# A fp32 decoder layer on one Trainium2 core: the FFN's two products as seven block products over pairs of token tiles, and its sample rows as plain fp32 products on four column strips

## The chip, the cores and the metric

The kernel runs on one core of a Trainium2 chip, as one launch. The metric is the device time of one execution in microseconds (us). Before the change it is 2831.03 us, the median of three runs (2824.38 to 2838.37). All inputs and outputs are fp32.

## The reference

One layer of a hybrid decoder for 2048 prompt tokens and 32 sample rows (8 requests of 4 tokens). A mixer (differential attention and retention on one normalised input) is followed by the FFN with which this case deals. Width D is 1024, D_FF is 2816.

```python
def swiglu(h, w_in_l, w_out_l):
    g, u = jnp.split(h @ w_in_l, 2, axis=-1)
    return (jax.nn.silu(g) * u) @ w_out_l

xp = xp + merge_head_groups(diff_o, ret_o, rg, ...)          # mixer, D wide
xp = xp + swiglu(rms_norm(xp, norm_ffn_g[l], NORM_EPS), w_ffn_in[l], w_ffn_out[l])
y_prompt = rms_norm(xp, norm_final_g, NORM_EPS)              # the same for xs, y_sample
```

## The kernel before

TensorE computes a fp32 product as **three fp32r products**. `split` (L114) makes two operands of one: `hi`, the fp32 value cast to fp32r by ACT (L116), and `lo`, what is left, by a DVE subtraction (L117). Then hi·hi, lo·hi and hi·lo are added up in PSUM.

The program has three stages. `projection` takes the input products of all rows (0 to about 600 us). `mixer` runs attention and retention over tiles of 128 tokens, and lays pieces of `out_rows` between attention pieces: for each tile it takes the out projection (L941 to L943), the residual, the FFN's norm (`stats`, `weigh`), and in `finish` turns the tile (four TensorE transposes into one PSUM tile, twice, in `turn`, L879), splits it and stores hi and lo to DRAM (`x2t_d`, POOL's queue, L975). `ffn` (L1014) is the rest.

`ffn` goes over four **groups of 512 tokens**; the fourth has the 32 sample rows too (544 columns, cut into two pieces of 272). For each group:

- `ffn_in` loads the group's hi and lo (L1041, POOL's queue). For each of 22 column tiles `f` of D_FF, and for gate and up, it loads 512 KB of weights (L1048, SP's queue), splits them, and takes 8 contraction steps `k` of three products (L1061): weights of 128x128 stand, 512 tokens move. SiLU is on ACT (L1066), the multiplication on DVE (L1067). The hidden rows `ht` stay in SBUF.
- `ffn_out` takes each half of the output's columns: for each `f` it loads 256 KB of weights, splits these and `ht`, and takes three products of 512 columns for each of four tiles of tokens (L1111 to L1113), which add up in four PSUM tiles over all 22 `f`. The sample rows go as one 64-row product of hi and lo together (`sample_terms`, L299). Residual (L1120), square (L1124), a power on POOL (L1156), scaling (L1157, L1158) and the store (L1161) follow for each tile. In the last group the last six `f` are held back, so that the tiles end one after the other.

A scheduler puts the order of the instructions of each engine down before the run, from the program's dependencies and a model of their times; buffers that run through rings (`bufs=`) set how far ahead a load or a split may go. The PSUM ring of the FFN has two pools of four.

The change and the prediction touch `out_rows`, `ffn`, `ffn_in`, `ffn_out` and the ring.

## Time and profile before

| | |
|---|---|
| runs | 2824.38, 2831.03, 2838.37 us |
| the profiled execution | 2826.33 us, of which the span from its first to its last instruction is 2824.6 us |
| granted TensorE clock, mean of the span | 0.997 |
| projection | 0 to about 600 us |
| mixer with `out_rows` | about 600 to 1246 us |
| FFN | about 1246 us to the end |
| DMA | 387.44 MB, mean 137 GB/s |

The page of the profile gives each engine's busy time and a strip of the span in 40 slices; its chain of waits follows the work that ended last back to the start. PE is the matrix engine (TensorE), DVE, ACT and POOL are the vector, scalar and GpSimd engines, SP is the queue that issues most loads. A matmul's own duration is not what it costs: matmuls overlap, and what counts is the distance from one start to the next, which the chain and the timeline show. Times at 1246 us and after belong to the FFN, apart from the last tiles of `out_rows`, whose products stand between the first FFN products up to about 1375 us.

### The profile page before, as it was taken

How to read it: one execution, taken by the hardware profiler on the slowest of the kernel's cores; microseconds unless marked ns; L12 is line 12 of the kernel's file. 1: busy time of each engine (PE TensorE's matmuls, PEld its weight loads, DVE VectorE, ACT ScalarE, POOL GpSimd, SP SyncE). 2: the span in 40 equal slices, each digit the busy share in tenths (PEclk: the TensorE clock that was granted, in tenths of full speed). 3: DMA queues.
4: the chain of work that ended last, by engine and by line, in shares of the span. 5: the costliest groups of instructions: out<-in, count | busy, mean ns of one | idle time of the engine just before them, and what ended most of it. 6: DMA issues, size and time to landing. Idle time of an engine off the chain costs nothing.

```text
span 2824.6 us, 37296 instructions
## 1 busy us (share of the span) xinstructions
PE 2777.2 (98%) x14584; PEld 2291.0 (81%) x14584; DVE 1296.6 (46%) x2198; ACT 1076.9 (38%) x2067; POOL 297.4 (11%) x421
## 2 busy tenths in 40 slices
PE   8999999999988999999999999999999999999998
PEld 7777788886667888888888888888888888999977
DVE  5454444444666776743322453224432235322254
ACT  4343343433565665642322442223432234322243
POOL 1000000004641221121000000000000000000000
PEclk9999999999999999999999999999999999999999
DMA  7436364356984766475633525335253342422122
GB/s 248 114 116 199 110 198 123 123 153 186 254 216 112 171 151 155 103 217 146 190 95 92 161 91 167 92 95 161 75 183 90 97 164 90 163 87 86 49 79 88
DMA packets 200784, 387.44 MB, mean 137 GB/s; under 512 B 20432, under 2 KB 88704, under 8 KB 200608
## 3 DMA queue, kind: packets, MB, share of 16 engines
q1 hardware_dynamic: 112240, 267.11, 30.2%
q0 software_dynamic: 79152, 113.75, 16.7%
q10 hardware_dynamic: 9216, 4.20, 0.6%
q8 instruction: 115, 1.88, 0.3%
q14 instruction: 61, 0.50, 0.1%
HBM read 311.72 MB, written 73.27 MB: 136 GB/s over the span
## 4 chain that ended last, share of the span: by engine, by line
PE 94%; ACT 2%; DVE 2%; DMA 1%; issue 1%; POOL 0%; ACTq 0%; POOLq 0%; SPq 0%
PE fps L1061 35%; PE z L290 6%; PE z L289 6%; PE z L288 6%; PE fps L1112 6%; PE fps L1113 6%; PE fps L1111 6%; PE op L840 4%; PE sp L782 2%; PE atp L829 2%; PE sp L785 2%; PE cz L941 2%; PE cz L942 2%; PE cz L943 2%; DMA cat<-cat_d 1%
## 5 line engine op out<-in xcount | busy, mean ns | idle before, releaser
L1061 PE MATMUL fps<-fx,fwh 128*128 128x512 f32 (+1 forms) x3520 | 896.3, 351 | 0.0
L1061 PEld LDWEIGHTS fps<-fx,fwh 128*128 128x128 f32 x3520 | 595.2, 188 | 94.7
L1061 PE MATMUL fps<-fx,fwl 128*128 128x512 f32 (+1 forms) x1760 | 562.0, 352 | 0.0
L116 ACT CAST fwh<-fwr 128x1024 fp32r<-128x1024 f32 x176 | 184.6, 1049 | 695.4 <-PE fps L1061 663.3
L117 DVE TENSOR_TENSOR fwl<-fwr,fwh 128x1024 fp32r<-128x1024 f32 x176 | 215.6, 1225 | 350.2 <-ACT fwh L116 342.6
L1061 PEld LDWEIGHTS fps<-fx,fwl 128*128 128x128 f32 x1760 | 308.0, 188 | 46.1
L288 PE MATMUL z<-wh,xh 128*128 128x512 f32 x768 | 303.6, 397 | 7.9 <-ACT xh L182 7.9
L290 PE MATMUL z<-wl,xh 128*128 128x512 f32 x768 | 304.4, 397 | 0.0
L289 PE MATMUL z<-wh,xl 128*128 128x512 f32 x768 | 302.8, 395 | 0.0
L1112 PE MATMUL fps<-vh,hl 128*128 128x512 f32 x680 | 263.4, 390 | 0.0
L1113 PE MATMUL fps<-vl,hh 128*128 128x512 f32 x680 | 263.2, 390 | 0.0
L1111 PE MATMUL fps<-vh,hh 128*128 128x512 f32 x680 | 206.1, 389 | 0.0
L786 DVE TENSOR_REDUCE mx<-sp 128x1 f32<-128x1024 f32 (+4 forms) x192 | 168.3, 907 | 70.3 <-PE sp L785 54.8
L1067 DVE TENSOR_TENSOR ht<-fps,sg 128x512 f32<-128x512 f32 (+1 forms) x110 | 63.0, 589 | 296.8 <-PE fps L1061 296.8
L117 DVE TENSOR_TENSOR vl<-vr,vh 128x512 fp32r<-128x512 f32 x170 | 117.1, 690 | 171.8 <-ACT vh L116 171.5
L116 ACT CAST vh<-vr 128x512 fp32r<-128x512 f32 x170 | 105.6, 622 | 201.3 <-PE fps L1112 195.7
L288 PEld LDWEIGHTS z<-wh,xh 128*128 128x128 f32 x768 | 145.0, 189 | 38.0 <-ACT xh L182 7.9
L290 PEld LDWEIGHTS z<-wl,xh 128*128 128x128 f32 x768 | 145.0, 189 | 31.8 <-issue 0.7
L289 PEld LDWEIGHTS z<-wh,xl 128*128 128x128 f32 x768 | 145.0, 189 | 31.2 <-issue 0.3
L117 DVE TENSOR_TENSOR wl<-wr,wh 128x1024 fp32r<-128x1024 f32 x96 | 117.3, 1223 | 110.3 <-ACT wh L116 109.9
L1111 PEld LDWEIGHTS fps<-vh,hh 128*128 128x128 f32 x680 | 127.6, 188 | 29.0
L782 PE MATMUL sp<-kst,qd 128*128 128x512 f32 (+1 forms) x320 | 125.8, 393 | 25.3 <-ACT p L800 19.3
(267 smaller groups left out, 3789.4 us busy)
## 6 DMA issues: line engine op xcount, KB each, us to landing
fwr<-w_ffn_in SPq DMA_DIRECT2D x176, 512.0 KB
wr<-w_in SPq DMA_DIRECT2D x96, 512.0 KB
vr<-w_ffn_out SPq DMA_DIRECT2D x176, 256.0 KB
kst<-k_d POOLq DMA_DIRECT2D x36, 512.0 KB
qd<-q_d POOLq DMA_DIRECT2D x64, 256.0 KB
fx<-x2t_d POOLq DMA_DIRECT2D x24, 512.0 KB
vv<-v_d SPq DMA_DIRECT2D x36, 256.0 KB
xr<-xt SPq DMA_DIRECT2D x16, 512.0 KB
```

The lines of the kernel that those rows point to most:

```text
L116: nc.scalar.copy(hi, src)
L117: nc.vector.tensor_tensor(lo, src, hi.bitcast(F32), ALU.subtract)
L288: mm(z, h[:, j, c], wh[:, j], start=k == 0, stop=False)
L289: mm(z, l[:, j, c], wh[:, j], start=False, stop=False)
L290: mm(z, h[:, j, c], wl[:, j], start=False, stop=k == KT - 1)
L782: nc.tensor.matmul(sp[:, o : o + nn], q[:, 2 * mp, sl], k, start=True, stop=False)
L786: nc.vector.tensor_reduce(mx[:, c : c + 1], sp[:, :w], AX.X, ALU.max, negate=True)
L840: self.nc.tensor.matmul(st["o"], ats[(b - lo) // 4][:, (b - lo) % 4, :], vs[b // 4][:, b % 4, :], start=b == 0, stop=b == st["i"],)
L1061: nc.tensor.matmul(pt[:, : c1 - c0], w[:, k], x[:, j, c0:c1], start=first, stop=last)
L1111: nc.tensor.matmul(o, hh[:, sl], vh, start=f == 0, stop=False)
L1112: nc.tensor.matmul(o, hl[:, sl], vh, start=False, stop=False)
L1113: nc.tensor.matmul(o, hh[:, sl], vl, start=False, stop=f == NF - 1)
```

## The change

The prompt's tokens are taken in pairs of 128-token tiles, even and odd. With X = [X11 X12; X21 X22] (rows: even and odd tile; columns: the two halves of the contraction) and W = [W11 W12; W21 W22], X·W comes from **seven block products instead of eight** (Winograd's form of Strassen's scheme):

- operands of X: X11, X12, X22 and the sums S1 = X21 + X22, S2 = S1 - X11, S3 = X11 - X21, S4 = X12 - S2; of W: W11, W21, W22 and four differences in the same manner
- products 0 to 6, each over half the contraction, then sums of the products for the four blocks of the result.

**FFN in** (`ffn_in`): two halves of 1024 tokens, four pairs each, so that 512 columns move as before. Columns of W are paired as gate and up. For each half, `x` has 28 tiles (7 operands, 4 contraction steps) of hi and lo, in SBUF for the whole half, with one buffer each; they are loaded raw through four single buffers `so0` to `so3` (L1102) and split. Their sums are made in `out_rows` (`sums`, POOL) and stored as fp32 (`xop_d`, SP's queue). For each `f` one load of 1 MB (ring `w` of 2), four POOL differences, seven splits into a ring of 8, and seven products of 4 steps by 3 terms (L1139). ACT, DVE and POOL add the products up. The column tiles are taken in pairs f = j and f = j + 11, whose hidden rows are the operands of FFN out; after each pair POOL makes four sums in `so0` to `so3` and stores seven operands (`hop_d`).

**FFN out** (`ffn_out`): for each of seven products in turn, 11 steps `j` of 8 pairs of tiles by 3 terms (L1302 to L1307), into 8 PSUM banks; each step loads 512 KB of `hop_d` and 256 KB of weights by SP and splits them. The differences of these weights (`top_d`) are made by POOL in the second half of FFN in (`second`), one `j` at a time. Each product ends with adds on DVE, ACT and POOL; the residual rows (`x2_d`) stay in SBUF.

**Sample rows**: for each `f` of the first half, 8 plain fp32 products of 32 rows by 256 columns, on four strips of 32 rows of the PSUM tile (`sample_in`), and two small products with a constant that adds the strips up and turns them (`sample_mid`); in `second`, four more on strips for FFN out.

The core of the diff, with pools, tile names and the plain loads cut:

```diff
@@ out_rows @@
         def finish(t):
...
-            hi = cr.tile([P, KT, P], F32R, tag="xhi", name="xhi", bufs=1)
-            lo = cr.tile([P, KT, P], F32R, tag="xlo", name="xlo", bufs=1)
+            xt = cr.tile([P, KT, P], F32, tag="xt", name="xt", bufs=2)
             for q in range(2):
-                self.turn(ps, r["xn"], m, q, hi, lo)
-            g = min(t // 4, 3)
-            c = P * t - 512 * g
-            for s, src in ((0, hi), (1, lo)):
-                nc.gpsimd.dma_start(self.x2t_d[g][s, :, :, c : c + m], src[:, :, :m])
+                tp = ps.tile([P, 4, P], F32, tag="t", name="ctp", bufs=2)
+                for j in range(4):
...
+                    nc.tensor.transpose(tp[:, j, :m], r["xn"][:m, c : c + P], self.ident[:m, :m])
+                dst = xt[:, 4 * q : 4 * q + 4, :m]
+                if q:
+                    nc.vector.tensor_copy(dst, tp[:, :, :m])
+                else:
+                    nc.scalar.copy(dst, tp[:, :, :m])
...
+            if t % 2 == 0:
+                self.even = xt
+                nc.sync.dma_start(d[0][:, :, c], xt[:, :half])
+                nc.sync.dma_start(d[1][:, :, c], xt[:, half:])
+                return
+            nc.sync.dma_start(d[3][:, :, c], xt[:, half:])
+            self.odd = (t, xt)
+
+        def sums():
...
+            tt = nc.gpsimd.tensor_tensor
+            tt(a22, a21, a22, ALU.add)
+            tt(a21, a11, a21, ALU.subtract)
+            tt(a11, a22, a11, ALU.subtract)
+            tt(a12, a12, a11, ALU.subtract)
+            for o, src in ((4, a22), (6, a21), (5, a11), (2, a12)):
+                nc.sync.dma_start(d[o][:, :, c], src)
@@ ffn_in @@
+            def operands(g):
...
+                for o in (0, 4, 5, 6, 1, 2, 3):
+                    for k in range(half):
+                        r = line(f"so{n % 4}")
+                        n += 1
+                        nc.sync.dma_start(r, self.xop_d[g][o][:, k, :])
...
+                        self.split(h, l, r)
...
+            def weights(w):
...
+                tt = nc.gpsimd.tensor_tensor
+                put(0, w11)
+                t1, t2, t3, t4 = (line("wt", 4) for _ in range(4))
+                tt(t1, w12, w11, ALU.subtract)
+                put(4, t1)
...
+            def sample_in(f, w):
+                z = psf.tile([P, 512], F32, tag="sz", name="sz", bufs=1)
+                for b in range(2):
+                    for q in range(4):
+                        k = 4 * b + q
+                        nc.tensor.matmul(
+                            z[32 * q : 32 * q + 32, : 2 * P].rearrange("p (s c) -> p s c", s=2),
+                            xs[:, k, :],
+                            w[:, :, k, :],
+                            start=b == 0,
+                            stop=b == 1,
+                        )
...
+            for g in range(2):
+                x = operands(g)
+                for j in range(NF // 2):
+                    hh = []
+                    for e in range(2):
+                        f = j + e * (NF // 2)
...
+                        ws = weights(w)
+                        ba, bb, bc_, bd = (ring.tile() for _ in range(4))
+                        product(0, ba, x, ws, True)
+                        c1 = line("c1")
+                        nc.scalar.copy(c1, ba)
+                        product(4, bc_, x, ws, True)
...
+                        if g == 0:
+                            z, zs = sample_in(f, w)
+                        product(5, bb, x, ws, True)
+                        u2 = line("u2")
+                        nc.vector.tensor_tensor(u2, bb, c1, ALU.add)
+                        product(6, bd, x, ws, True)
+                        u3 = line("u3")
+                        nc.vector.tensor_tensor(u3, bd, u2, ALU.add)
+                        nc.gpsimd.tensor_tensor(c5, u3, c5, ALU.add)
+                        if g == 0:
+                            sample_mid(f, z, zs)
+                        product(1, ba, x, ws, False)
...
+                        product(2, bc_, x, ws, False)
...
+                        product(3, bd, x, ws, False)
...
+                    so = [line(f"so{n}") for n in range(4)]
+                    tt = nc.gpsimd.tensor_tensor
+                    tt(so[0], h21, h22, ALU.add)
+                    tt(so[1], so[0], h11, ALU.subtract)
+                    tt(so[2], h11, h21, ALU.subtract)
+                    tt(so[3], h12, so[1], ALU.subtract)
+                    d = self.hop_d[j]
+                    for o, src in enumerate((h11, h12, so[3], h22, so[0], so[1], so[2])):
+                        nc.gpsimd.dma_start(d[o][:, g, :], src)
+                    if g == 1:
...
+                        self.second(fw, line, j, acc)
+    def second(self, fw, line, j, acc):
...
+        for n in range(2):
+            for e in range(2):
+                q = 2 * n + e
+                nc.tensor.matmul(
+                    acc[32 * q : 32 * q + 32, :],
+                    self.hs[:, j + e * (NF // 2), :],
+                    w[:, e, 512 * n : 512 * n + 512],
...
+        tt(t[0], w12, w11, ALU.subtract)
+        tt(t[1], w22, t[0], ALU.subtract)
+        tt(t[2], w22, w12, ALU.subtract)
+        tt(t[3], w21, t[1], ALU.subtract)
+        for n in range(4):
+            nc.gpsimd.dma_start(self.top_d[j][:, n, :], t[n])
@@ ffn_out @@
+            def operands(o, j):
+                xr = fo.tile([P, 2, 512], F32, tag="xr", name="xr", bufs=3)
+                nc.sync.dma_start(xr, self.hop_d[j][o])
+                wr = fo.tile([P, 512], F32, tag="wr", name="wr", bufs=4)
...
+                x = self.halves(fo, xr.rearrange("p g t -> p (g t)"), 1024, ("xh", "xl"), 4)
+                return *x, *self.halves(fo, wr, 512, ("vh", "vl"), 4)
...
+            for o, fresh in ((0, True), (1, False), (5, True), (4, True), (2, False), (6, True), (3, False)):
+                if fresh:
+                    banks = [ps.tile([P, 512], F32, tag="ps", name="ops") for _ in range(8)]
...
+                for j in range(nj):
+                    parts = operands(o, j)
+                    if o == 3 and j >= nj - last:
+                        held.append((j, parts))
+                        continue
+                    for p in range(8):
+                        product(banks[p], p, *parts, fresh and j == 0, j == nj - 1)
...
+                    if o == 0:
+                        nc.scalar.copy(u, b)
+                    elif o == 1:
+                        add(xa[p][:, lo], b, xa[p][:, lo], ALU.add)
+                    elif o == 5:
+                        add(u, b, u, ALU.add)
+                        padd(xa[p][:, hi], u, xa[p][:, hi], ALU.add)
...
```

How the rows of the engines move, at three places. Names carry a number of the buffer; a row's end is the size of the result.

First **PE where `out_rows` ends and the FFN begins**: before, the first rows of the FFN (`fps`, L1061) stand among the out projections (`cz`) and the turning (`ctp`) of the last tiles:

```order
L943 MATMUL cz_11331<-wol7_6663,chi_11300 128x512
L879 MATMUL ctp_11375<-ident_84,xn_11273 128x128 x4
L879 MATMUL ctp_11422<-ident_84,cat_11327 128x128 x4
L1061 MATMUL fps_12019<-fx00_11997,fwh_12015 128x512
L1061 MATMUL fps_12050<-fx00_11997,fwh_12046 128x512
L1061 MATMUL fps_12085<-fx00_11997,fwh_12081 128x512
L941 MATMUL cz_11384<-woh0_5496,chi_11300 128x512
L942 MATMUL cz_11384<-woh0_5496,clo_11301 128x512
L943 MATMUL cz_11384<-wol0_5497,chi_11300 128x512
```

After, the last out projection and the last turning stand ahead of the first row of the FFN (L1139):

```order
L947 MATMUL cz_12026<-woh7_6764,chi_11968 128x512
L948 MATMUL cz_12026<-woh7_6764,clo_11969 128x512
L949 MATMUL cz_12026<-wol7_6765,chi_11968 128x512
L979 MATMUL ctp_12060<-ident_180,xn_12054 128x128 x4
L979 MATMUL ctp_12066<-ident_180,xn_12054 128x128 x4
L1139 MATMUL fps_12313<-xh00_12109,wh_12277 128x512
L1139 MATMUL fps_12473<-xh00_12109,wh_12437 128x512
L1139 MATMUL fps_12313<-xl00_12110,wh_12277 128x512
L1139 MATMUL fps_12313<-xh00_12109,wl_12278 128x512
L1139 MATMUL fps_12313<-xh01_12115,wh_12277 128x512
L1139 MATMUL fps_12473<-xl00_12110,wh_12437 128x512
```

Before, 264 rows of the out projections of the last tiles follow the first row of the FFN; after, none does, and the first two `f` run side by side.

Second, **POOL during FFN in**. Before, it issues the loads of a group's operands and takes the powers of the norm:

```order
L1041 DMA fx12_14525<-x2t_d1_76 128x2x512
L1041 DMA fx02_14523<-x2t_d1_76 128x2x512
L1041 DMA fx13_14529<-x2t_d1_76 128x2x512
L1041 DMA fx03_14527<-x2t_d1_76 128x2x512
L1156 TENSOR_TENSOR fss_13967<-fss_13967,half_90 128x1
```

After, in the second half of the tokens (`wt` the weights' differences, `so` the sums of hidden rows, L1253 to L1258 `second`):

```order
L1129 TENSOR_TENSOR wt_17255<-w_17246,wt_17253 128x512
L1253 TENSOR_TENSOR wt_17413<-w2_17406 128x512
L1216 TENSOR_TENSOR so1_17068<-so0_17067,h00_16902 128x512
L1221 DMA hop_d2_4_108<-so0_17067 128x512
L1254 TENSOR_TENSOR wt_17414<-w2_17406,wt_17413 128x512
L1258 DMA top_d3_170<-wt_17413 128x512
L1255 TENSOR_TENSOR wt_17415<-w2_17406 128x512
L1218 TENSOR_TENSOR so3_17070<-h10_17047,so1_17068 128x512
L1221 DMA hop_d2_5_109<-so1_17068 128x512
L1195 TENSOR_TENSOR c5_17169<-u3_17197,c5_17169 128x512
L1258 DMA top_d3_170<-wt_17414 128x512
```

So POOL has sums of 512 columns that it did not have, and the stores are issued between them.

Third, **SP at the boundary of the two halves of tokens**. Before, its rows at such a place are loads of the next weights and of what FFN out needs. After:

```order
L1102 DMA so0_15960<-xop_d1_0_82 128x512
L1102 DMA so2_16116<-xop_d1_3_85 128x512
L1102 DMA so1_15966<-xop_d1_0_82 128x512
L1102 DMA so0_15984<-xop_d1_4_86 128x512
L1102 DMA so3_15978<-xop_d1_0_82 128x512
L1102 DMA so1_15990<-xop_d1_4_86 128x512
L1102 DMA so0_16008<-xop_d1_5_87 128x512
L1102 DMA so3_16002<-xop_d1_4_86 128x512
```

The operands of the second half pass through the same four single buffers in which POOL makes the sums of hidden rows.

More of the change, by code (lines that the diff above doesn't have):

```diff
@@ L1002, in out_rows @@
             yield
+            sums()
             product(t, 1, range(4, 8))
@@ L1012, in out_rows @@
         yield
+        sums()
     def ffn(self):
[L1015 to L1030 removed]
@@ new lines, in ffn, with pool @@
+        tc, nc, a = self.tc, self.nc, self.a
+        with ExitStack() as st:
+            def pool(name, **k):
+                return st.enter_context(tc.tile_pool(reuse_waits="tile", name=name, **k))
+            fs = pool("fs", bufs=1, side="right")
+            self.hs = fs.tile([P, NF, NS], F32, name="hs")
+            self.comb = fs.tile([P, NS + P], F32, name="strips")
+            nc.gpsimd.dma_start(self.comb, a["strips"])
+            self.ysum = fs.tile([NS, D], F32, name="ysum")
+            self.ffn_in()
+            self.ffn_out()
@@ new lines, in second @@
+    def second(self, fw, line, j, acc):
+        nc, a = self.nc, self.a
+        w = fw.tile([P, 2, D], F32, tag="w", name="w2", bufs=2)
+        for e in range(2):
+            nc.sync.dma_start(w[:, e, :], a["w_ffn_out"][j + e * (NF // 2)])
+        for n in range(2):
+            for e in range(2):
+                q = 2 * n + e
+                nc.tensor.matmul(
+                    acc[32 * q : 32 * q + 32, :],
+                    self.hs[:, j + e * (NF // 2), :],
+                    w[:, e, 512 * n : 512 * n + 512],
+                    start=j == 0,
+                    stop=j == NF // 2 - 1,
+                )
+        w11, w12, w21, w22 = w[:, 0, :512], w[:, 0, 512:], w[:, 1, :512], w[:, 1, 512:]
+        t = [line("wt", 4) for _ in range(4)]
+        tt = nc.gpsimd.tensor_tensor
+        tt(t[0], w12, w11, ALU.subtract)
[4 more added lines that the diff above has]
+            nc.gpsimd.dma_start(self.top_d[j][:, n, :], t[n])
@@ L1187, with __init__ @@
 class _Ring:
-    def __init__(self, *pools):
-        self.pools, self.n, self.first = pools, 0, True
+    def __init__(self, four, three):
+        self.pools, self.n = [four] * 4 + [three] * 3, 0
     def tile(self):
-        pool = self.pools[0 if self.first else self.n // 4 % 2]
+        n = self.n % 7
         self.n += 1
-        return pool.tile([P, 512], F32, tag="ps", name="fps")
+        return self.pools[n].tile([P, 512], F32, tag="ps", name="fps", bufs=4 if n < 4 else 3)
 class _Tag:
@@ L1258, in tables @@
     c["dsel"] = ds
+    st = np.zeros((P, NS + P), f)
+    st[p, p % NS] = 1.0
+    for n in range(2):
+        st[p, NS + NS * n + p % NS] = p // (2 * NS) == n
+    c["strips"] = st
     c["piota"] = np.arange(P, dtype=f)[:, None]
```

325 lines of the change are left out of this document (180 added, 145 removed).

## Prediction

> **What bounds the kernel now.** I read the page first, then the chain, then windows of the FFN.
>
> ```profile
> span 2824.6 us, 37296 instructions
> ...
> PE 2777.2 (98%) x14584; PEld 2291.0 (81%) x14584; DVE 1296.6 (46%) x2198; ACT 1076.9 (38%) x2067; POOL 297.4 (11%) x421
> ...
> GB/s 248 114 116 199 110 198 123 123 153 186 254 216 112 171 151 155 103 217 146 190 95 92 161 91 167 92 95 161 75 183 90 97 164 90 163 87 86 49 79 88
> ...
> PE 94%; ACT 2%; DVE 2%; DMA 1%; issue 1%; POOL 0%; ACTq 0%; POOLq 0%; SPq 0%
> ```
>
> PE is busy for 98% of the span, and 94% of the chain of waits is PE's. Busy spans overlap on PE, so I check stage by stage. The windows give the length, then busy time and instructions of PE, PEld, DVE, ACT and POOL, the granted clock, the DMA share and GB/s.
>
> ```profile
> 1040.00:1240.00 200.00, 199.11 (x1281) 172.31 (x1280) 141.75 (x223) 121.33 (x267) 35.73 (x56) 1.00 0.56 144
> 1372.00:1562.00 190.00, 190.00 (x821) 153.47 (x820) 58.31 (x60) 48.15 (x60) 6.00 (x9) 1.00 0.42 125
> 1562.00:1682.00 120.00, 120.00 (x531) 99.31 (x530) 59.79 (x96) 49.90 (x91) 1.40 (x2) 1.00 0.38 119
> 1684.00:1927.00 243.00, 243.00 (x1048) 196.28 (x1047) 75.94 (x82) 64.89 (x84) 6.48 (x10) 1.00 0.39 122
> 2412.00:2676.00 264.00, 264.00 (x2105) 263.80 (x2104) 79.97 (x114) 68.36 (x115) 2.47 (x4) 1.00 0.32 102
> 2815.00:2825.00 10.00, 2.27 (x10) 1.07 (x8) 3.32 (x7) 2.89 (x6) 1.07 (x2) 0.81 0.25 93
> ```
>
> Up to the tail PE has no gap in the FFN, at a granted clock of 1.00. DVE (75.94 of 243) and ACT (64.89) are far from full, POOL is idle. So the FFN's time is its number of matmuls by their spacing, and a matmul removed is worth one spacing. The chain and PE's timeline give it (start, length, what):
>
> ```profile
> 1628.76 2.31 PE fps L1061 x10
> ...
> 1684.60 242.19 PE fps L1061 x1043
> ```
>
> ```profile
> 2413.22 262.82 PE fps L1061 x2098
> ```
>
> ```profile
> 1561.70 0.39 PE L1111 MATMUL fps<-vh,hh 128*128 128x512 f32 x1
> ...
> 1565.79 0.39 PE L1111 MATMUL fps<-vh,hh 128*128 128x512 f32 x1
> ```
>
> A group of FFN in has 22x2x8x3 = 1056 matmuls of 512 columns. Ten were taken early, so 242.19 us are 1046 matmuls: **0.2315 us** each (the trace lacks three records). The fourth group, 2112 of 272 columns, takes **262.8 us**. In FFN out, 18 matmuls lie between the two starts: 4.09/18 = **0.2275 us**.
>
> **What goes.** FFN in: 3 groups x 1056 x 0.2315 = 733.4, and 262.8. FFN out: 4 groups x 2 halves x 22 f x 4 tiles x 3 = 2112 by 0.2275 = 480.5. Sample rows of FFN out: 88 by the same = 20.0. Together 1496.7 us.
>
> **What comes on PE.** FFN in: 2 halves x 22 f x 7 products x 4 steps x 3 terms = 3696 of 512 columns, x 0.2315 = 855.6. FFN out: 7x11x8x3 = 1848 x 0.2275 = 420.4. For the sample rows the decode part has the same forms:
>
> ```profile
> 736.47 1.92 PE L612 MATMUL dop<-pg,dat 128*32 128x512 f32 x16
> 738.32 0.50 PE L782 MATMUL sp<-kst,qd 128*128 128x512 f32 x1
> ```
>
> ```profile
> 690.50 1.34 PE L543 MATMUL dsn<-ks_t,qb 128*128 128x32 f32 x8
> 691.77 0.41 PE L557 MATMUL dsp<-pg,qb 128*32 128x128 f32 x2
> ```
>
> A plain fp32 product leaves two records. So eight strip products of 512 columns on four strips took 738.32 - 736.47 = 1.85 us; eight of 256 columns take half, 0.93. Four products of 32 columns took 1.27, two 0.64. Per f that is 1.57, by 22 = 34.5; four strip products of 512 columns in each of 11 `second` are 11 x 0.93 = 10.2; the two at the end about 1. Sum added: 855.6 + 420.4 + 45.7 = 1321.7.
>
> **Gain on PE: 1496.7 - 1321.7 = 175.0 us.**
>
> **What must stay under PE.** A pair of column tiles (f = j, j + 11) has 168 matmuls: 38.9 us of PE. With samples this is 42.0 us in the first half; in the second, 39.8.
>
> ```profile
> L117 DVE TENSOR_TENSOR vl<-vr,vh 128x512 fp32r<-128x512 f32 x170 | 117.1, 690 | 171.8 <-ACT vh L116 171.5
> ...
> L116 ACT CAST vh<-vr 128x512 fp32r<-128x512 f32 x170 | 105.6, 622 | 201.3 <-PE fps L1112 195.7
> ```
>
> DVE has 14 split subtractions and 12 further 512-column operations a pair: 26 x 0.69 = 18 us. ACT has 14 casts and 8 others: 22 x 0.62 = 14 us. In FFN out, one step of 24 matmuls is 5.46 us of PE against DVE's 3 x 0.69 and ACT's 3 x 0.62. Its loads are 768 KB, so 144 GB/s; the strip of GB/s above has slices at 248 and 254. All of this is covered.
>
> **POOL** is the engine whose load is new. It gets 14 sums of 512 columns and 7 stores a pair in the first half, 18 and 11 in the second.
>
> ```profile
> L517 POOL MEMSET qb<- 128x1024 f32 x1 | 1.0, 951 | 0.0
> ...
> L111 POOL TENSOR_SCALAR nss<-nss 128x4 f32<-128x4 f32 x16 | 5.7, 357 | 91.9 <-ACT njunk L902 91.9
> ```
>
> ```profile
> L695 POOL DMA_DIRECT2D qd<-q_d x64 | 35.2, 563 | 52.8 <-PE sp L785 52.1 <-PE atp L829 0.6
> L975 POOL DMA_DIRECT2D x2t_d<-xhi x17 | 15.4, 904 | 130.0 <-ACT xhi L116 130.0
> L112 POOL TENSOR_TENSOR css<-css,half 128x1 f32<-128x1 f32 x16 | 8.9, 558 | 1.4
> L111 POOL TENSOR_SCALAR css<-css 128x1 f32<-128x1 f32 x16 | 3.0, 190 | 9.6 <-ACT xn L957 9.6
> ```
>
> No row shows a sum of 512 columns on POOL. Lower end: the memset writes 1024 columns in 0.951, so 0.48 for 512. Upper end: from one column to four, TENSOR_SCALAR grows from 190 to 357 ns, 56 ns a column, 28 us for 512. The memset is the nearer row, as the only wide one. A sum reads two streams and writes one, so I take three times 0.48 = **1.4 us**. A store's issue I take as 0.65, between 0.563 and 0.904. First half: 14 x 1.4 + 7 x 0.65 = 24.2 of 42.0. Second: 18 x 1.4 + 11 x 0.65 = 32.4 of 39.8. Covered, but with a margin of only a fifth.
>
> The Trainium skill, page "GPSIMD Engine Reference", section "3.1 Elementwise — side-by-side cycle accounting", speaks against placing sums there: elementwise work is to go to DVE, since GpSimd needs 4497 ns for an addition of 2048 fp32 columns. An estimate from it for 512 is 1.12 us, and POOL's second half would be 27.4 of 39.8; no run here shows it yet.
>
> **What the change opens on PE** (working values, with their ends):
>
> ```profile
> L963 DVE SCALAR_TENSOR_TENSOR xn<-xres,css,gf 128x1024 f32<-128x1024 f32 x16 | 20.5, 1279 | 5.5 <-POOL css L112 5.5
> ...
> L957 ACT ACTIVATE xn<-xres 128x1024 f32<-128x1024 f32 x16 | 17.0, 1061 | 24.9 <-issue 18.0 <-DVE xres L949 6.9
> ```
>
> ```profile
> 1238.26 4.50 DMA cat<-cat_d
> ```
>
> - **Start of the FFN, +18 (5 to 40).** PE no longer has FFN products between the last tiles. Each of the last four exposes a cast, a subtraction and their signals, about 1.7, so 7. The last tile then has residual 0.69, square 1.06, POOL 0.19 + 0.56, weighing 1.28, two copies and a turning, some 6 in all after what still runs. Its four POOL sums (5.6), store and reload (a landing took 4.50) stand before product 4's operands, and only product 0 of two f's (5.6) covers them: 5.
> - **Boundary of the token halves, +16 (5 to 35).** SP's reloads through `so0` to `so3` wait until POOL has made and stored the last pair's sums there. After the last product: DVE 0.69, SiLU 0.62, DVE 0.69, two sums and some issues 4.8, a store 3, a reload 3, a split 1.3, less the little that is ready. Behind these SP has the next loads, which PE needs later. Then each product of two f's (24 x 0.2315 = 5.6 us) asks for four operands, whose line cycle of about 4.7 is shorter.
> - **FFN in to FFN out, +5 (0 to 12):** the first `hop_d` and weights are long stored; gfin, residual rows and new pools come.
> - **Six changes of product in FFN out, +6 (0 to 12):** each bank is read by one copy or add (0.69) before it is restarted. Where the next product adds to the bank, nothing waits.
> - **Tail, +1 (0 to 4);** attention, where SP's stores of sums stand ahead of its loads, **+2 (0 to 12)**.
> - **Small waits for POOL and DVE, +8 (0 to 25):** weights' differences stand in order among `hop_d` sums and stores, and a split behind a late one holds up a product.
> - **Clock, +5 (0 to 15).** Where PE has gaps the granted clock is lower:
>
> ```profile
> 650.00:700.00 50.00, 43.91 (x248) 32.89 (x247) 21.18 (x68) 14.77 (x50) 15.38 (x18) 0.93 0.57 170
> ...
> 2820.00:2824.60 4.60, 0.00 (x0) 0.00 (x0) 0.74 (x1) 0.72 (x1) 0.54 (x1) 0.63 0.12 29
> ```
>
> Sum of losses: 61. **Result:** the profiled execution took 2826.3 us (span 2824.6), 4.7 below the median of 2831.03, inside the runs' spread. 2826.3 - 175.0 + 61 = 2712, rounded to **2710 us**. The losses' ends add up to 10 and 155; that all lie at one end is unlikely, and I take 25 to 110. With 25, and FFN in at FFN out's spacing (3696 x 0.004 = 15 less), it is 2661; with 110, 2761.
>
> **Rivals.**
>
> A. *DVE and POOL block each other.* A pair has 18 DVE operations with both inputs in SBUF (14 subtractions, 4 products of SiLU or sums): 12.4 us. If POOL's sums wait for these, POOL's second half is 25.2 + 12.4 + 7.2 = 44.8 against 39.8, so 11 x 5.0 = +55: **2765**. The first half, 36.6 of 42, still fits. Against it: in 1040 to 1240 DVE is busy 141.75 of 200 and POOL 35.73, and PE keeps 199.11; but POOL reads little there. The Trainium skill, page "SBUF — State Buffer", section "Who interferes with whom", has such a lock: a DVE instruction with two SBUF inputs contends with a GpSimd instruction that reads SBUF. No run here shows it so far. Chance 0.20.
>
> B. *POOL becomes the bound, and the kernel is slower.* Place: the weights' differences of FFN in, without which product 4 does not start. With d the time of a sum, the second half is bound from 18d + 7.2 > 39.8, d = 1.8, the first from 14d + 4.6 > 42, d = 2.7. The gain of 114 is gone at d = 2.4. At d = 3 the cost is 11 x (21.4 + 4.6) = +286: **2998**. For it: 56 ns a column, and 558 ns for a power of one column. Against: those are narrow rows where fixed cost rules; the memset is wide and fast. Chance 0.12.
>
> C. *The strips do not run side by side.* Each would take 3.7 for four, so 33 products of this kind cost 2.8 more: +91, **2803**. The L612 row speaks against it: it is this form. Chance 0.04.
>
> That the change does less than it says: the counts of matmuls are fixed by the loops, so only their cover is open, which A and B are.
>
> **How the numbers follow.** The forecast has 0.64, A 0.20, B 0.12, C 0.04. The range 2655 to 2805 holds the forecast's own ends, A and C; left out are B and a tail of the forecast. About 0.5% (14 us) is what a measurement can tell from no change. Faster by more holds for forecast, A and most of C, and for B at d below 2.3: 0.84. The same: 0.04, a narrow strip of B. Slower: 0.12.
>
> **What would show it.** PE's spacing in FFN in 0.2275 to 0.2315; POOL's sums near 1.4 us, under 1.8; POOL busy about 80% of the second half (B: 100%, PE waiting for `wt` or `wl`; A: sums of uneven length, longer while DVE runs L117); PE idle about 18 us before the first FFN product and 16 at the boundary; eight strip products in 0.93 us. The prediction is wrong if PE idles in every pair, if the spacing of the matmuls changes with seven operands in turn, or if the boundaries cost several times what I gave them.

## The result and the profile after

The changed kernel takes **2729.01 us** (median of four runs, 2727.98 to 2735.78), before 2831.87 in the same session: a ratio of **0.9643, with a 95% interval of 0.9614 to 0.9671**. The forecast was 2710, range 2655 to 2805. The profiled execution took 2728.34 us, with a span of 2726.6; before, the span was 2824.6, so 98.0 us went.

From the page, the first lines:

```profile
span 2726.6 us, 35659 instructions
...
PE 2616.8 (96%) x13180; PEld 2092.6 (77%) x13180; DVE 1568.0 (58%) x2296; ACT 1061.8 (39%) x2051; POOL 950.8 (35%) x991
```

PE is busy 160.4 us less, but no longer without gaps. Its page's chain of waits cannot be followed back to the start in this trace (PE has only 28% of the span in it), so I read windows. The columns are again length; busy time and instructions of PE, PEld, DVE, ACT, POOL; granted clock; DMA share; GB/s.

```profile
1246.00:1338.00 92.00, 79.14 (x353) 62.46 (x351) 41.33 (x57) 24.84 (x61) 40.77 (x44) 0.93 0.48 155
1338.00:1400.00 62.00, 53.02 (x215) 36.07 (x216) 39.98 (x56) 29.13 (x53) 22.17 (x18) 0.91 0.52 168
1400.00:1800.00 400.00, 400.00 (x2010) 318.05 (x2009) 216.56 (x291) 126.76 (x232) 227.62 (x206) 1.00 0.28 97
...
1816.00:1875.00 59.00, 39.32 (x145) 27.06 (x144) 34.28 (x42) 22.85 (x40) 24.96 (x23) 0.86 0.57 190
1875.00:2270.00 395.00, 394.62 (x1763) 317.78 (x1762) 308.08 (x263) 124.70 (x219) 297.64 (x289) 1.00 0.44 153
...
2282.00:2319.00 37.00, 37.00 (x164) 30.60 (x164) 13.73 (x15) 9.64 (x13) 11.44 (x21) 1.00 1.00 376
2319.00:2330.00 11.00, 0.41 (x3) 0.01 (x1) 0.17 (x2) 2.14 (x4) 2.89 (x2) 0.61 0.44 169
2330.00:2713.00 383.00, 383.00 (x1679) 316.93 (x1680) 183.43 (x203) 131.71 (x181) 61.91 (x45) 0.99 0.47 153
```

The two long stretches of FFN in (400 and 395 us) and FFN out after 2330 are as full as the FFN was before. Apart from the passage from FFN in to FFN out and the tail, PE is idle in four places: at the last tiles of `out_rows`, in the first 62 us of FFN in, at the boundary of the token halves (about 1816 to 1875), and once in FFN out, at 2319.

Of the 2010 records in 1400 to 1800, 1613 are FFN matmuls; the sample rows of 20 column tiles take about 27 us (below), so the spacing is (400 - 27)/1613 = 0.2313 us. In 1875 to 2270, 1689 are FFN matmuls, and nine `second` of 1.0 us each lie among them: (395 - 9)/1689 = 0.2285. The last row has 383/1679 = 0.2281, but its first 5 us stand at half the clock (next section); in the variant e4, whose FFN out has no stop, 1848 matmuls take 419.0 us, 0.2267 each. The sample rows on PE's timeline, with the FFN's next row behind each:

```profile
1508.11 1.07 PE L1153 MATMUL sz<-w,xs 128*32 128x256 f32 x16
1509.12 0.50 PE L1139 MATMUL fps<-xh,wh 128*128 128x512 f32 x1
...
1514.73 0.53 PE L1167 MATMUL sz<-strips,zs 128*128 128x32 f32 x4
1515.09 0.48 PE L1139 MATMUL fps<-xh,wh 128*128 128x512 f32 x1
```

Eight strip products take 1.01 us (0.93 was forecast), the two small ones 0.36 (0.64).

For the comparisons below I cut the FFN at PE's own instructions: the time from the 1st to the 200th matmul of FFN in (**start**), from the 1700th to the 2000th (**boundary**), from the 2000th to the 3600th (**steady**), and from the first to the last matmul of FFN out (**out**). By the spacings and the sample rows without any wait, start would be 50.0, boundary 72.7, steady 375 and out 419. The whole FFN is counted from its first matmul to the end of the span: the stages ahead of it scatter. In the 13 profiled executions of the changed kernel and its variants the FFN began between 1332.2 and 1352.7 us, though no edit was aimed at that. Medians of two variants that differ by less than some 10 us are therefore not told apart by their ratios; the parts of the FFN, each from the one profiled execution, are the firmer comparison. Start scatters too: 64.7 to 71.5 us in variants whose edits were not aimed at it.

| kernel | median us | ratio to before | start | boundary | steady | out | FFN |
|---|---|---|---|---|---|---|---|
| changed | 2729.01 | 0.9643 (0.9614 to 0.9671) | 68.9 | 101.1 | 374.7 | 432.0 | 1388.4 |
| e1_late_norm | 2729.81 | 0.9661 (0.9639 to 0.9683) | 67.1 | 100.1 | 375.1 | 431.8 | 1385.8 |
| e4_norm_tied | 2719.56 | 0.9625 (0.9599 to 0.9651) | 68.0 | 99.1 | 375.4 | 418.8 | 1373.2 |
| e2c_ring_six | 2723.20 | 0.9631 (0.9608 to 0.9654) | 64.7 | 99.7 | 383.5 | 419.4 | 1379.0 |
| e2_own_lines | 2717.75 | 0.9613 (0.9589 to 0.9637) | 65.0 | 79.6 | 385.4 | 430.8 | 1372.5 |
| e3_start | 2733.07 | 0.9664 (0.9641 to 0.9687) | 61.2 | 102.0 | 376.8 | 432.5 | 1386.2 |
| e8_out_eight | 2757.53 | 0.9752 (0.9727 to 0.9777) | 66.0 | 76.6 | 374.9 | 485.3 | 1414.4 |
| e6_twice | 2832.17 | 1.0012 (0.9998 to 1.0025) | 71.5 | 105.8 | 466.1 | 431.5 | 1486.7 |
| e7_dve_diffs | 2732.57 | 0.9665 (0.9639 to 0.9691) | 68.3 | 99.9 | 375.6 | 432.5 | 1388.0 |
| e5_both | 2713.70 | 0.9591 (0.9561 to 0.9621) | 67.1 | 85.2 | 383.3 | 420.9 | 1367.8 |
| e9_best | 2724.26 | 0.9636 (0.9613 to 0.9660) | 68.6 | 88.5 | 386.1 | 420.6 | 1375.7 |
| e11_best_dve | 2716.75 | 0.9589 (0.9573 to 0.9605) | 69.5 | 85.8 | 373.7 | 420.9 | 1362.0 |
| **e12_best_dve_all** | **2705.30** | **0.9552 (0.9533 to 0.9572)** | 68.4 | 81.7 | 373.7 | 420.0 | 1355.6 |

### The profile page after: what moved, and what is told of

Its sections match the earlier page's. It is cut to its first block, busy times and chain, and to the rows that moved or that the text cites. A ratio compares the mean times of both kernels' runs of the same rounds, so it can differ in the third digit from the quotient of the medians.

```text
span 2726.6 us, 35659 instructions
## 1 busy us (share of the span) xinstructions
PE 2616.8 (96%) x13180; PEld 2092.6 (77%) x13180; DVE 1568.0 (58%) x2296; ACT 1061.8 (39%) x2051; POOL 950.8 (35%) x991
## 5 line engine op out<-in xcount | busy, mean ns | idle before, releaser
L1139 PE MATMUL fps<-xh,wh 128*128 128x512 f32 x1232 | 486.9, 398 | 20.0 <-ACT xh L122 19.6
L1139 PE MATMUL fps<-xl,wh 128*128 128x512 f32 x1232 | 483.3, 393 | 3.4 <-DVE xl L123 3.4
L1139 PE MATMUL fps<-xh,wl 128*128 128x512 f32 x1232 | 481.0, 391 | 0.0
L1139 PEld LDWEIGHTS fps<-xh,wh 128*128 128x128 f32 x1232 | 232.5, 189 | 89.9 <-ACT xh L122 25.3
L1139 PEld LDWEIGHTS fps<-xl,wh 128*128 128x128 f32 x1232 | 232.7, 189 | 57.0 <-DVE xl L123 9.3
L1139 PEld LDWEIGHTS fps<-xh,wl 128*128 128x128 f32 x1232 | 232.6, 189 | 49.3 <-issue 0.4
L123 DVE TENSOR_TENSOR wl<-wt,wh 128x512 fp32r<-128x512 f32 x176 | 218.4, 1246 | 77.7 <-ACT wh L122 73.1
L1305 PE MATMUL ops<-vh,xh 128*128 128x512 f32 x616 | 234.1, 391 | 12.7 <-ACT xh L122 10.6
L1305 PE MATMUL ops<-vh,xl 128*128 128x512 f32 x616 | 239.3, 391 | 0.0
L1305 PE MATMUL ops<-vl,xh 128*128 128x512 f32 x616 | 239.1, 390 | 0.0
```

The source lines that it names most:

```text
L123: nc.vector.tensor_tensor(lo, src, hi.bitcast(F32), ALU.subtract)
L1139: nc.tensor.matmul(bank, w[:, c], v, start=first and k == 0 and n == 0, stop=k == half - 1 and n == 2, skip_group_check=True,)
L1305: nc.tensor.matmul(bank, x[:, c], w, start=first and n == 0, stop=end and n == 2, skip_group_check=True)
```

## The experiments

### The stop in FFN out (e1, e4)

The chain of waits of the changed kernel at 2300 to 2335 (start, length, what):

```profile
2297.29 18.32 DMA x<-x_d
...
2315.89 9.47 DMA xsr<-x_d
...
2325.50 2.34 POOL xsr L1352
...
2328.82 0.18 ACT y L1285
2329.01 0.94 ACT xh L122
...
2329.99 5.06 PE ops L1305 x11
```

Read backwards: PE waits for a split on ACT. That split stands behind ACT's square of the sample rows' result; this waits for an addition on POOL, and this for a small load, which stands in POOL's queue behind the loads of 16 residual tiles (8 MB). Nothing in FFN out needs the sample rows' result.

PE starts nothing for 10.97 us, 10.7 more than a spacing, and the stop costs more than that. Behind it the granted clock is 0.50 for 5 us, and the eleven matmuls of the last row take 5.06 us, where at 0.2267 they would take 2.5:

```profile
2329.90:2335.00 5.10, 5.01 (x12) 3.94 (x13) 5.03 (x5) 3.16 (x6) 0.00 (x0) 0.50 0.44 137
```

e1 wrote the block of the sample rows one product later:

```diff
-                if o == 0:
+                if o == 1:
                     xs = fo.tile([NS, D], F32, name="xsr")
```

> Edit: the norm of the 32 sample rows (load of x2_d's sample rows, POOL add, norm) stands behind product 1 of FFN out, not behind product 0. Theory: PE's stop of 10.97 us in product 0 (2319.0 to 2330.0 in the changed kernel) is ACT waiting in order for POOL's add, which waits for a load queued behind the 16 residual loads; ACT's next instruction is the split that PE needs. So the stop goes and the time falls by about 11 us, to 2718 (2714 to 2722). Rival: the splits' own loads (xr, wr) are late because the 8 MB of residual rows fill the DMA engines (DMA share 1.00 from 2282 to 2319); then the stop stays, at 8 us or more, with ACT or PE waiting for xr or wr, and the time stays at 2729.

The stop stayed, 11.49 us. But ACT's order had not changed: the scheduler had put the block at the same place, since nothing in its dependencies kept it back. So e1 tells nothing of either theory. e4 gave it a dependency, by a ring of buffers that is used before:

```diff
-                if o == 0:
-                    xs = fo.tile([NS, D], F32, name="xsr")
+                if o == 2:
+                    xr_s = fo.tile([P, D], F32, tag="y", name="xsr", bufs=3)
+                    xs = xr_s[:NS]
```

> Edit: the sample rows' residual is loaded into the ring of y tiles, after the first eight norms, so that its load, POOL's add and ACT's square cannot stand before product 2 of FFN out. In the run e1 the same block, only written later, stood at the same place on ACT, and the stop stayed (11.49 us). Theory: that order on ACT is the whole cause of the stop; FFN out from its first to its last matmul falls from 432.0 to about 421 us, and the time by about 11, to 2718 (2713 to 2722). Rival: DMA engines filled by the residual rows (share 1.00) make the splits' loads late; then the stop stays in part, 5 us or more, and FFN out takes 426 us or more.

Out fell from 432.0 to 418.8, the 10.7 of the stop and the 2.5 behind it; the median fell to 2719.56. All of FFN out in e4:

```profile
2273.00:2692.00 419.00, 418.96 (x1848) 346.77 (x1848) 198.87 (x221) 144.96 (x198) 78.46 (x69) 1.00 0.54 178
```

The sample rows' chain ahead of the split on ACT was the cause. The full DMA engines (share 1.00, 376 GB/s in the row from 2282) alone stop nothing: PE ran through them. They count only in that the small load had to wait behind the residual rows.

### The boundary of the token halves (e2, e2c)

From the timelines of PE, SP and POOL in the changed kernel:

```profile
1817.05 1.06 PE L1243 MATMUL sacc<-w,hs 128*32 128x512 f32 x6 [0.22 <-DMA w<-w_ffn_out]
1830.61 0.80 PE L1139 MATMUL fps<-xh,wh 128*128 128x512 f32 x1 [12.51 <-ACT xh L122]
```

```profile
1815.18 32.41 SPq L1102 DMA_DIRECT2D so<-xop_d  x17
```

```profile
1819.34 1.63 POOL L1215 TENSOR_TENSOR so<-h,h 128x512 f32<-128x512 f32 x1 [0.74 <-DVE h L1210]
...
1823.27 1.27 POOL L1218 TENSOR_TENSOR so<-h,so 128x512 f32<-128x512 f32 x1
```

POOL makes the last pair's sums in `so0` to `so3` up to 1824.5, and 17 operand loads of the second half take SP's queue until 1847.6. PE waits 12.51 us for the first split, and several times later. e2 gave the loads lines of their own; SBUF had no room, so the ring of split weights went from 8 to 6. e2c changed the ring alone.

```diff
-                        r = line(f"so{n % 4}")
+                        r = line(f"xo{n % 4}")
...
-                    h, l = self.halves(fw, src, 512, ("wh", "wl"), 8)
+                    h, l = self.halves(fw, src, 512, ("wh", "wl"), 6)
```

> Edit: the raw operand loads of FFN in go through four lines of their own (xo0 to xo3), not through so0 to so3; to make room the ring of split weights is 6 deep, not 8. Theory: the loss of about 28 us around the boundary of the token halves (1800 to 1875) comes from reloads that wait until the last pair's hidden sums have left the shared lines; with own lines the operands of the first products are loaded and split under the last pair, and the boundary costs 2 to 10 us: the time falls by 18 to 26 us, to about 2707 (2702 to 2712). Rival: the single buffers of the split operands (xh, xl) or DMA bandwidth set the pace there; then 20 us or more of PE's gap stay and the time is within 6 us of 2729.

> Edit: the ring of split weights is 6 deep, not 8, and nothing else. It is the counterpart of the run with own lines. Theory: PE is full in steady FFN in with 8 and the splits run well ahead, so 6 costs nothing: 2729 within 6 us. Rival: seven splits are needed per column tile, and with 6 PE waits in every tile; then 0.3 to 1 us per tile, 44 tiles, 13 to 44 us more.

The boundary went from 101.1 (99.7 in e2c) to 79.6: the shared lines cost 20 us, about the 18 to 26 expected. The whole FFN fell only by 16, since steady became 385.4 and the stop in FFN out stayed; so the time missed the 2702 to 2712 expected. In e2c the FFN fell by 9 against the changed kernel, for a reason that was not expected: the scheduler placed the sample rows' load ahead of the residual rows, so the stop of FFN out was gone there (419.4). Its time lies within what was expected by luck, for the theory that a ring of 6 costs nothing was wrong: steady took 9 more (why, under e9).

### The start of FFN in (e3)

```profile
1349.03 1.50 PE L1153 MATMUL sz<-w,xs 128*32 128x256 f32 x11 [5.63 <-DMA xs<-xs_d]
```

```profile
1346.55 0.61 POOL L1089 DMA_DIRECT2D xs<-xs_d  x1
```

```profile
1342.59 4.55 SPq L1013 DMA_DIRECT2D xop_d<-xt  x4
1347.24 2.08 SPq L1102 DMA_DIRECT2D so<-xop_d  x4
```

PE waits for the sample rows' load, which POOL issues behind the last tile's sums; SP issues the next operand loads behind the stores of these sums. e3 swapped the queues:

```diff
-                nc.sync.dma_start(d[o][:, :, c], src)
+                nc.gpsimd.dma_start(d[o][:, :, c], src)
...
-            nc.gpsimd.dma_start(xs, self.xs_d)
+            nc.sync.dma_start(xs, self.xs_d)
```

> Edit: POOL's queue, not SP's, stores the four sums of a pair of tiles; SP's queue, not POOL's, loads the sample rows of FFN in. Theory: of the 19 us lost from 1338 to 1400, most is SP's operand loads (first half of the tokens, whose operands were stored long before) standing in order behind the stores of the last pair's sums, and the sample rows' load standing in order behind POOL's sums. With both gone PE's gap of 6.0 us at 1343 closes and the later ones shrink: the time falls by 8 to 18 us, to about 2716 (2711 to 2721). Rival: the pace is set by the four single lines through which 28 operands are loaded and split; then the gaps move but the sum stays, and the time is within 5 us of 2729.

Start fell by 7.7 us to 61.2, just short of the 8 to 18 expected, and only 3.5 below the shortest start of the variants not aimed at it (64.7). PE's wait for the sample rows is gone, but the whole FFN fell only by 2.2, and the median did not fall: the expectation was missed. As a change of the kernel this is no gain.

### FFN out as eight products (e8)

```diff
-                    tt(so[0], h21, h22, ALU.add)
...
-                    for o, src in enumerate((h11, h12, so[3], h22, so[0], so[1], so[2])):
+                    for o, src in enumerate((h11, h12, h21, h22)):
...
-            for o, fresh in ((0, True), (1, False), (5, True), (4, True), (2, False), (6, True), (3, False)):
+            for o in range(8):
+                fresh = o % 2 == 0
...
```

> Edit: FFN out as eight block products (the plain ones) on the same pairs of tiles, loops and loads; hidden sums and the differences of its weights are left out, and products of one block add up in one bank. FFN in keeps its seven. Theory: the gain of FFN out is only its 264 matmuls by their spacing, 264 x 0.2278 = 60.1 us, and what its seven cost beside that (POOL's sums and stores, more adds at the ends) is covered: 2729 + 60 = 2789 (2780 to 2795), FFN out 432 -> 492 us, second half of FFN in unchanged. Rival: the sums and stores for the seven do cost PE; then FFN in gets faster by 5 us or more and the time is below 2780.

Out grew by 53. Without the stops and the slow matmuls behind them (13.2 in the changed kernel, 6.6 in e8, which has a shorter stop) it is 60, as the count of 264 matmuls says. But the boundary fell by 24.5, to 76.6: without hidden sums the four lines are free, and the boundary is as short as with lines of their own (e2). The median is **28.5 us above the changed kernel's, not 60**. So the seven products of FFN out pay back half of what they save, at the boundary and in the stop, and none of it in the steady stretch (374.9 against 374.7).

### POOL and DVE (e6, e7)

POOL's groups in the changed kernel, and three DVE lines (minimum/median/maximum in ns):

```profile
L1123 POOL TENSOR_TENSOR wt<-w,wt 128x512 f32<-128x512 f32 x44 | 68.1, 1547 | 4.6 <-DVE wl L123 1.9
...
L1121 POOL TENSOR_TENSOR wt<-w 128x512 f32<-128x512 f32 x44 | 58.0, 1318 | 183.9 <-DMA w<-w_ffn_in 171.4 <-DVE wl L123 8.1 <-DVE u L1194 4.4
L1221 POOL DMA_DIRECT2D hop_d<-so x88 | 48.8, 555 | 3.0 <-POOL so L1217 3.0
```

```profile
L123 DVE TENSOR_TENSOR wl<-wt,wh x176: 673/929/3819, 1251.3 to 2257.6; 128x512 fp32r<-128x512 f32 x176
```

```profile
L1203 DVE TENSOR_TENSOR h<-fps,u x44: 675/682/692, 1388.2 to 2272.5; 128x512 f32<-128x512 f32 x44
```

```profile
L1204 DVE TENSOR_TENSOR h<-sg,h x44: 676/684/2426, 1389.4 to 2273.3; 128x512 f32<-128x512 f32 x44
```

A sum on POOL takes 1.3 to 1.55 us, near the 1.4 that was taken (means of the two rows). But the subtractions on DVE, 0.69 before, now take up to 3.8 us. L1203 reads one operand from PSUM and never takes longer than 0.692; L1204, of the same size with both in SBUF, takes up to 2.43. At one place of the timelines, DVE and then POOL:

```profile
1810.53 1.68 DVE L123 TENSOR_TENSOR wl<-w,wh 128x512 fp32r<-128x512 f32 x1
1813.82 1.33 DVE L123 TENSOR_TENSOR xl<-so,xh 128x512 fp32r<-128x512 f32 x1 [1.62 <-ACT xh L122]
...
1815.68 0.67 DVE L123 TENSOR_TENSOR wl<-wt,wh 128x512 fp32r<-128x512 f32 x1
```

```profile
1810.01 1.65 POOL L1123 TENSOR_TENSOR wt<-w,wt 128x512 f32<-128x512 f32 x1
1811.62 1.73 POOL L1195 TENSOR_TENSOR c<-u,c 128x512 f32<-128x512 f32 x1
1813.31 1.29 POOL L1125 TENSOR_TENSOR wt<-w 128x512 f32<-128x512 f32 x1
1816.50 1.60 POOL L1129 TENSOR_TENSOR wt<-w,wt 128x512 f32<-128x512 f32 x1 [1.89 <-DVE wl L123]
```

The two long ones lie on POOL's sums; the third, in POOL's pause from 1814.6 to 1816.5, takes 0.67. This is rival A's lock, and the Trainium skill, page "SBUF — State Buffer", section "Who interferes with whom", has it as the trace shows it: two SBUF inputs on DVE contend with a GpSimd instruction that reads SBUF, one does not.

e6 made each of the weights' differences twice, e7 made them on DVE:

```diff
-                tt = nc.gpsimd.tensor_tensor
+                def tt(*k):
+                    nc.gpsimd.tensor_tensor(*k)
+                    nc.gpsimd.tensor_tensor(*k)
```

```diff
-                tt = nc.gpsimd.tensor_tensor
+                tt = nc.vector.tensor_tensor
```

> Edit: POOL makes each of the four weights' differences of FFN in twice, with the same result: 8 sums more per pair of column tiles. Theory (forecast's row: POOL is covered with a quarter to spare): in the second half POOL is busy 75% of 39.9 us a pair (29.9 us); 8 x 1.44 = 11.5 us more make 41.4, over PE's 39.8 by 1.6, 11 pairs: +18 us; in the first half, 57% of 42, they fit. DVE is held longer behind POOL as well, so +18 to +60: 2747 to 2790. Rival (POOL is far from the bound, or its busy time overlaps in a way the page doesn't show): the time stays within 8 us of 2729.

> Edit: DVE, not POOL, makes the four weights' differences of FFN in. In the changed kernel DVE's split subtraction wl, both inputs in SBUF, takes 1.24 us on the mean (0.67 to 3.93) and DVE's h = PSUM + u, one input in SBUF, 0.68 (0.68 to 0.69). Theory: the first waits while POOL runs a sum, so with 8 of POOL's 14 to 18 sums a pair gone the mean of wl falls below 1.0 us; POOL's busy share of the second half falls from 75% to about 50%; DVE does 8 x 0.69 = 5.5 us a pair more and stays under PE; the steady stretch (matmuls 2000 to 3600) stays 374 to 377 us and the time 2729 within 8 us. Rival: the long subtractions are due to DVE's own input (split weights arriving late from ACT or memory), then wl stays above 1.1 us.

The window of e6's second half:

```profile
1900.00:2375.00 475.00, 412.11 (x1718) 320.28 (x1719) 334.89 (x257) 122.39 (x214) 396.43 (x356) 0.93 0.36 124
```

e6 lost **103 us**, not 18 to 60, and took away the whole gain. Steady is 466.1 for 1600/168 = 9.5 pairs, 48.9 us a pair, though POOL is busy only 396 of 475 us. POOL's busy time is the wrong bound. In this window PE waits 43.6 us for `wl` of DVE and 17.6 for `wh` of ACT, and its granted clock is 0.93. If POOL's sums and DVE's two-input operations add up, a pair has 26 x 1.28 + 18 x 0.69 = 45.7, against PE's 39.8. By the same count the changed kernel has 18 x 1.28 + 12.4 = 35.4: it fits, with 11% to spare. This count is an argument that comes near the 48.9, not a measurement: the two engines overlap in part, and the clock has a share in the loss. In e7 the median of `wl` fell to 0.69 (685 and 692 ns in its two groups), its mean from 1.24 to 1.04 us, short of the "below 1.0" expected; steady and time stayed, as PE was full there before.

### Together (e5, e9, e11, e12)

e5 put the boundary and the stop together, with three lines for the loads, one hidden sum made in place of an operand, and a ring of 7. e9 kept the ring's 8, by sending the sample rows' result of FFN out through DRAM.

```diff
-                        r = line(f"so{n % 4}")
+                        r = line(f"xo{n % 3}")
...
-                    so = [line(f"so{n}") for n in range(4)]
+                    so = [line(f"so{n}") for n in range(2)] + [h21, line("so2")]
...
```

```diff
-            self.ysum = fs.tile([NS, D], F32, name="ysum")
...
-                nc.scalar.copy(self.ysum[:, 512 * n : 512 * n + 512], z[:NS])
+                zz = line(("u2", "u3")[n])
+                nc.scalar.copy(zz[:NS], z[:NS])
+                nc.gpsimd.dma_start(self.ysum_d[:, 512 * n : 512 * n + 512], zz[:NS])
...
```

> Edit: as in e4, and the operand loads go through three lines of their own; room for them comes from one hidden sum made in place, and a ring of split weights 7 deep, not 8. Theory: both losses go and add up: boundary 101.1 -> about 80 us (matmuls 1700 to 2000 of FFN in), FFN out 432.0 -> about 421, nothing lost to the ring of 7 (374.7 -> 374 to 378 from 2000 to 3600). FFN from its first matmul to the end: 1388.4 -> about 1357; the time about 2698 (2692 to 2706). Rival: with 7 the ring holds one column tile only and PE waits as with 6 (+10 us), and three lines are too few; then about 2710.

> Edit: as e5_both (operand loads through three lines of their own, one hidden sum in place, the sample rows' norm tied behind product 2), but the ring of split weights keeps its 8; room comes from the sample rows' result of FFN out, which goes through DRAM instead of staying in SBUF. Theory: the boundary (matmuls 1700 to 2000) is about 80 to 85 us as with own lines, the steady second half 375 as with a ring of 8 (383 with 7), FFN out 419 to 421; FFN from its first matmul to the end about 1388 - 17 - 12 = 1359, the time 2700 (2694 to 2707). Rival: the loss in the steady second half came not from the ring but from the shifted order of POOL's work, and stays at 383; then 2708 or more.

Boundary and out did what was expected, within 5 us. Steady did not, and so both times were missed: 383.3 and 386.1, **with a ring of 8 as with 7**. So a shorter ring is not needed for this loss. The timelines of e9 show what it is, DVE, POOL and PE:

```profile
2040.52 5.04 DVE L124 TENSOR_TENSOR wl<-wt,wh 128x512 fp32r<-128x512 f32 x1
2045.48 0.68 DVE L1194 TENSOR_TENSOR u<-fps,u 128x512 f32<-128x512 f32 x1
```

```profile
2039.97 1.31 POOL L1129 TENSOR_TENSOR wt<-w,wt 128x512 f32<-128x512 f32 x1
2041.22 1.29 POOL L1255 TENSOR_TENSOR wt<-w 128x512 f32<-128x512 f32 x1
2042.47 1.29 POOL L1216 TENSOR_TENSOR so<-so,h 128x512 f32<-128x512 f32 x1
2043.72 1.28 POOL L1217 TENSOR_TENSOR h<-h,h 128x512 f32<-128x512 f32 x1
2044.95 0.56 POOL L1221 DMA_DIRECT2D hop_d<-so  x1
```

```profile
2046.21 0.50 PE L1139 MATMUL fps<-xh,wh 128*128 128x512 f32 x1 [1.33 <-DVE u L1194]
```

Four sums follow one another on POOL without a pause. A subtraction of DVE that began with them ends when POOL turns to a DMA; then comes `u`, for which PE waits 1.33 us. PE waits like this, 1.2 to 1.6 us, in six pairs of that half. Such waits for `u` account for what steady lost in e2c (four) and e2 (five), and for half of it in e5 (three); the longest subtractions took 6.6, 7.6 and 7.7 us there. The changed kernel has one such wait, of 0.4 us, and no subtraction above 3.8. The changed kernel has as many sums a pair as e9, 18; what differs is their order. e11 and e12 break up the runs, and take sums away from POOL as well: e11 is e9 with e7's edit, e12 also makes the differences in `second` on DVE.

> Edit: as e9_best, and the four weights' differences of FFN in are made by DVE, as in e7. In e9 one subtraction wl on DVE took 5.04 us (2040.5 to 2045.5), as long as four POOL sums stood one behind the other without a gap, and PE stopped for 1.3 us after it, waiting for DVE's u; such a stop came in most pairs of the second half (386.1 us for matmuls 2000 to 3600, against 374.7). Theory: DVE is held for as long as POOL's sums follow without a gap; with 8 fewer sums a pair the runs are short and the stops go: 375 to 377 for that stretch, boundary 80 to 86, FFN out 420; FFN from its first matmul to the end about 1362 (1356 to 1368), the time 2700 (2693 to 2710). Rival: the shifted order of loads and splits itself costs the 10 us; then the stretch stays at 383 or more and the time at 2710 or more.

> Edit: as e11, and DVE also makes the four differences of FFN out's weights (second). POOL keeps 6 sums a pair and the stores. Theory: with the stops gone in e11 this changes nothing more: within 4 us of e11, POOL's busy share of the second half from about 50% to about 38%, DVE's to 75% at most. Rival: DVE, with 38 operations of 0.69 us a pair, holds up the additions that free PE's banks, and the stretch of matmuls 2000 to 3600 grows by 5 us or more.

Steady is 373.7 in both, as the theory has it, and the rival, that the shifted loads and splits themselves cost the 10 us, is out. No run changes the order alone with all 18 sums on POOL. The window of e12's second half:

```profile
1865.00:2240.00 375.00, 375.00 (x1682) 301.15 (x1681) 293.88 (x371) 121.44 (x212) 138.51 (x166) 1.00 0.44 156
```

POOL is busy for 37% of it. e11's FFN is the 1362 expected, but its time lies above the expected range: its FFN began the latest of all, at 1352.7. e12's median is 11 us below e11's, where 4 was expected; 6.4 of that is FFN (1362.0 to 1355.6, most of it at the boundary), the rest the scatter ahead of it. e12 beats both kernels: **2705.3 us**, 0.9552 of before (0.9533 to 0.9572, against 0.9614 to 0.9671 for the changed kernel).

## Why the prediction was right, and where its sizes were off

The mechanism was right: matmuls taken from a full PE were worth their spacing, and most of the losses stood where they were looked for; the stop in FFN out did not. The sizes were off on both sides, by 11 us in the gain and 27 in the losses, and that the two partly cancel is luck.

- **The gain on PE** was forecast at 175.0. By the measured spacings 1848 x (0.2313 + 0.2285 + 0.2267) = 1268.7, and 42.4 for sample rows (22 x 1.37 + 11 x 1.0 + 1.3), make 1311.1 added; against 1496.7 removed that is 185.6.
- **The losses** were forecast at 61 and are 88: this is the term that was mis-sized.
  - Start: 18 was forecast, 36.7 measured. Before, the FFN's 1496.7 and the 7.5 behind its last matmul taken from the span leave 1320.4; FFN in begins at 1338.2, 17.8 later, and loses 18.9 more (68.9 - 50.0). Two queues were named, but only one wait of 5 us was priced. The first part carries the scatter of the earlier stages.
  - Boundary: 16 was forecast, 28.4 measured. The place and the cause were right (e2); the wait for the later operands, which the forecast saw as covered, was not: behind the first wait PE waits 6.9 us more, in eight places, for splits of operands.
  - The six changes of product: 6 forecast, nothing measured (e4's FFN out is 1848 matmuls by 0.2267). In their place stood a stop that the forecast did not have, the sample rows' norm on ACT's queue: 10.7, and 2.5 at half the clock.
  - Into FFN out 3.5 for 5. Tail 5.8 for 1: 13.3 us stand behind the last matmul, 7.5 before, where twelve products of the sample rows ran beside the last tile's norm.
  - Small waits for POOL: 8 forecast, one of 0.4 in the steady stretch. POOL was busy for 75% of it, where about 80% was forecast.
  - Clock: the 5 that were forecast have no row of their own; the lower clock (0.91 at the start, 0.86 at the boundary, 0.50 behind the stop) is in the terms above. The 2 for attention can't be told from the scatter.
  - 185.6 - (36.7 + 28.4 + 3.5 + 13.2 + 5.8) = 98.0, and the spans differ by 98.0. Each term is good to some 2 us only, so that it closes so well is chance.
- **Rival A** was half right. The lock is there, but it lengthens DVE's operations more than POOL's, and its sum of 44.8 took 1.4 us a sum and counted issues in; with 1.28 and no issues it is 35.4, under 39.8. It did not set the time of the changed kernel, but it held PE up when POOL's sums stood in a row (e9), and by the count above when 8 sums were added (e6).
- **Rival B** was off: sums of 1.3 to 1.55 us lie under its 1.8. Its bound was the wrong one all the same: e6 lost far more than POOL's busy time gives.
- **Rival C** was wrong: eight strip products took 1.01 us.
- Two slips in the forecast's numbers change little: 4.09/18 is 0.2272, not 0.2275 (0.6 us over FFN out), and beside forecast, A and C with 0.88, rival B's 0.12 can't hold both "the same" with 0.04 and "slower" with 0.12.

What stays open: why the stages ahead of the FFN scatter by some 20 us from one profiled execution to another. It was not tried. Open too are most of the 36.7 us at the start, of which e3 took one wait away, and the size of e6's loss beyond the count.

## What to carry to other kernels

Fewer matmuls on a full PE are worth their spacing (e8: 60 us for 264, with the stops taken out); what decides is where their new operands pass. Look for buffers that two stages share (here four lines, 20 us) and for instructions of no urgency that stand ahead of urgent ones on an in-order engine (13 us with the slow clock behind the stop), and tie such an instruction to something late, since writing it later need not move it. Where POOL and DVE both read two operands from SBUF, add their times up instead of looking at each one's busy share (e6), and look for sums of POOL that follow one another without a pause (e9), which the total does not show.

## What the runs showed of the hardware that was not expected

A DVE operation with two SBUF inputs can be held through several sums of POOL: the one shown took 5.04 us across four of them, 0.69 alone. Mostly it is let in after one. Between 1880 and 2270 us, 96 of 176 such operations of 512 columns in the changed kernel lay across the end of one sum, 18 of two, nine of three and none of four; in e9 it was 92, 17, one and nine of 166. What lets it in is open. POOL's sums also grow, from 1.28 to 1.6 to 1.7 us, where DVE's two-input operations run. An estimate from the Trainium skill, page "GPSIMD Engine Reference", section "3.1 Elementwise — side-by-side cycle accounting", was 1.12 for 512 columns, and the traces have 1.28; its advice to keep such sums on DVE agrees with e9 to e12 (2724 to 2705 us), while e7, the same step taken on the changed kernel, gained nothing (2733 against 2729).
